# Later norm products, squares and weight sums at the start of the MLP's up projection; first down weights in another buffer and the last convolution behind them

## The chip, the cores and the metric

The kernel runs on one core of a Trainium2 chip. The metric is the device time of one execution in microseconds (us). TensorE is called PE here, its weight loads PEld, VectorE DVE, ScalarE ACT, GpSimd POOL; SP is the queue that issues nearly all DMAs. All engines run side by side, each through its own instructions in a fixed order, and wait for each other by semaphores.

## The reference, cut to what matters

One decoder layer runs on 1024 prompt tokens and 8 single new tokens, 1032 columns in all. Its first part (a norm, an input projection, two recurrent mixers, an output projection and the residual add, giving `x`) is touched only at its very end. Its second part is a gated MLP:

```
def rmsnorm(x, w):
    y = x * rsqrt(mean(x * x, axis=-1) + EPS)
    return y * w

x = x + concat([o_a, y]) @ w['w_out']            # 2048 -> 1024
h = rmsnorm(x, w['norm2_w'])
gate, val = split(h @ w['w_up'], 2)              # 1024 -> 2 x 2816
gate, buf = causal_dwconv(gate, buf_f, w['ffn_conv_w'], w['ffn_conv_b'])   # width 3
x = x + (silu(gate) * val) @ w['w_down']         # 2816 -> 1024
```

All of it is float32.

## The kernel before

**Layout.** Channels lie on the 128 partitions and tokens on the free axis, so `x` is 8 tiles of 128 x 1032. The tokens are cut into two halves of 516 columns, each of two quarters of 258 (`QW`). A float32 product is made of three rounded ones (high x high, low x high, high x low), so every operand has to be split first: ACT rounds it into a high tile (`wh`, `uh`, `ah`) and DVE subtracts to get the low tile (`wl`, `ul`, `al`).

**End of the output projection.** `out_job` (L1197) adds four products to `x` for each pair of channel tiles `m`; in the last pass over the second half DVE writes the finished piece `y_` into a small tile (tag `us`, a pool of 10 buffers), and `final` (L1248) stores it, squares it on ACT and adds the square to `rst` (tile `n2r`) on POOL. `rst` holds the sum of squares of each token over the 8 channel tiles.

**Norm.** `set_norm(i, c)` (L1307) sums `rst` over the partitions for one quarter by a PE product with ones (tile `n2ms`), and turns it into the reciprocal root with one ACT and three DVE instructions (L736 to L739). For the second half the scale is not put on the operands: it is multiplied onto the up projection's results (`p4` on DVE, `p3` on POOL).

**Up projection.** It runs in 22 steps `j` (`FT`), one for each 128 gate and 128 value channels. Each step uses a Strassen-like scheme of 7 products (`p1` to `p7`) for each token half, 12 matmuls to a product. The operands of a half, sums and differences of `x` quarters, are made once by `set_of(i)` (L1320): `comb` adds, `put` rounds and subtracts (L1349, L1350). The weights of a step are loaded by `up_load` (L1403), which also makes four sums of them (L1419, tile `wt`; POOL from step 1 on), and are split by `up_split` (L1428). `Up.p1` to `Up.p7` take the results out of PSUM; `p4` of a half may have to wait there for `p7`. `up_close` (L1513) then runs the convolution of width 3 (`conv_tail`, one ACT and two DVE instructions of 1048 columns, L354 and L356), the SiLU on ACT, and the product with `val`, and stores the step's result to DRAM (`act_d`).

**Order.** PE's instructions stand in the order in which the program issues them. All others are put into their queue by a list scheduler that works from the emission order, so a change in the emission moves rows on several engines. `tick()` is called after each matmul; `after(n, work)` emits `work` n matmuls later; `spread` emits the pieces of a generator at intervals of n matmuls. Step 0 (`ups(0, ...)`) runs all 7 products of the first half and then all 7 of the second, in the order `FIRST` = p1, p2, p4, p6, p5, p7, p3; the second half's operands are still being made while it runs. Later steps alternate the halves in the order p1, p6, p5, p7, p2, p4, p3.

**PSUM.** Products p1, p7, p3 (tiles `ua`) use 3 banks; p2, p4, p6, p5 (tiles `ub`) and one of the norm products use 4 others. A product waits until the bank it is given has been emptied.

**Down projection.** `act_load` (L1558) brings a stored result back (SP) and splits it. For each group of `RND` = 4 of the 22 channel tiles and each pair of output tiles, `wload` (L187) loads 512 KB of `w_down` into `ws`, rounds to `wh` (L199) and subtracts to `wl` (L201); then 8 products of 12 matmuls each (tile `dn`) follow, each added to its `x` tile by DVE (L1601). The tags `wh` and `wl` exist with two buffers each in two pools, `tmp` and `wpool`: in a step `up_split` uses `tmp` for its first two pairs of weights and `wpool` for its last two, and `wload` uses `wpool`.

## Time and profile before

| what | value |
|---|---|
| runs | 1733.5, 1734.27 (median), 1738.18 us |
| profiled execution, its own time | 1734.45 us |
| its span (first to last instruction) | 1732.7 us |
| mean granted PE clock | 0.994 |
| output projection ends, up step 0 begins | 999.4 us |
| up step 1 begins | about 1029.7 us |
| down projection begins | 1454.9 us |

The span is cut into 40 equal slices below; a digit is the busy share in tenths, PEclk the clock that was granted to PE in tenths.

```profile
## 2 busy tenths in 40 slices
PE   7999999999999999999999989999999998999997
...
DVE  6667756565575555466655877666766677444445
ACT  7567686345364444446334554334333334111114
POOL 2102132120121112011232367666666662000002
```

The slice is 43.3 us long, so the digits 8 on PE stand at 996 to 1040 us (start of the up projection) and at 1429 to 1473 us (start of the down projection). DVE's largest digits stand in the first of these.

### The profile page before, as it was taken

To read this page: it belongs to the slowest core of one execution; us is meant where nothing else is said; L and a number is where in the kernel's file an instruction comes from. 1 tells how busy PE (TensorE), PEld (TensorE's weight loads), DVE (VectorE), ACT (ScalarE), POOL (GpSimd) and SP (SyncE) were. 2 spreads that over 40 slices of the span, in tenths; PEclk is the share of its full clock that TensorE was granted. 3 is DMA by queue.
4 is the path that set the end of the run, shared out by engine and by line. 5 is a ranking of instruction groups with operands and counts; after the bars stand their busy time and mean duration, and the time that the engine had idled before them with its cause. 6 is when DMAs were issued, how large, how long until landed. Compare 5 with 4: busy or idle time off the path is not lost. (4 is left out here: it accounts for less than half of the span.)

```text
span 1732.7 us, 38321 instructions
## 1 busy us (share of the span) xinstructions
PE 1698.1 (98%) x16056; PEld 1654.6 (95%) x16056; DVE 1084.4 (63%) x1968; ACT 777.6 (45%) x1432; POOL 489.8 (28%) x503
## 2 busy tenths in 40 slices
PE   7999999999999999999999989999999998999997
PEld 7899998999999999999999989999999998999997
DVE  6667756565575555466655877666766677444445
ACT  7567686345364444446334554334333334111114
POOL 2102132120121112011232367666666662000002
PEclk9999999999999999999999999999999999999999
DMA  5354334643434334426358612222222227322212
GB/s 169 66 129 112 105 92 141 174 132 99 130 89 136 114 93 129 122 90 198 113 154 273 210 57 87 74 75 74 86 82 91 74 74 273 102 68 94 81 61 99
DMA packets 251000, 200.22 MB, mean 116 GB/s; under 512 B 48029, under 2 KB 222613, under 8 KB 250810
## 3 DMA queue, kind: packets, MB, share of 16 engines
q1 hardware_dynamic: 250538, 197.67, 37.5%
q8 instruction: 126, 2.06, 0.5%
q14 instruction: 48, 0.39, 0.1%
q0 software_dynamic: 288, 0.10, 0.0%
HBM read 155.16 MB, written 46.95 MB: 117 GB/s over the span
## 5 line engine op out<-in xcount | busy, mean ns | idle before, releaser
L93 PE MATMUL mm<-hl,wh 128*128 128x344 f32 x1248 | 405.1, 325 | 0.3 <-issue 0.3
L93 PE MATMUL mm<-hh,wh 128*128 128x344 f32 x1248 | 404.9, 325 | 0.0
L93 PE MATMUL mm<-hh,wl 128*128 128x344 f32 x1248 | 401.9, 322 | 0.0
L93 PEld LDWEIGHTS mm<-hl,wh 128*128 128x128 f32 x1248 | 235.4, 189 | 4.7 <-issue 4.2
L93 PEld LDWEIGHTS mm<-hh,wh 128*128 128x128 f32 x1248 | 235.5, 189 | 3.1 <-issue 2.5
L93 PEld LDWEIGHTS mm<-hh,wl 128*128 128x128 f32 x1248 | 235.6, 189 | 1.8 <-issue 1.7
L199 ACT CAST wh<-ws 128x1024 fp32r<-128x1024 f32 x96 | 100.6, 1048 | 247.7 <-PE dn L93 138.0
L93 PE MATMUL ub<-uh,wh 128*128 128x258 f32 x704 | 200.7, 285 | 1.5 <-DVE nt L737 0.8
L93 PE MATMUL ub<-ul,wh 128*128 128x258 f32 x704 | 199.7, 284 | 0.0
L93 PE MATMUL ub<-uh,wl 128*128 128x258 f32 x704 | 199.3, 283 | 0.0
L93 PE MATMUL dn<-ah,wl 128*128 128x256 f32 (+1 forms) x640 | 181.2, 283 | 5.8 <-DVE wl L201 5.8
L93 PE MATMUL dn<-ah,wh 128*128 128x256 f32 (+1 forms) x640 | 181.6, 284 | 0.0
L93 PE MATMUL dn<-al,wh 128*128 128x256 f32 (+1 forms) x640 | 180.7, 282 | 0.0
L201 DVE TENSOR_TENSOR wl<-ws,wh 128x1024 fp32r<-128x1024 f32 x88 | 115.4, 1312 | 95.1 <-ACT wh L199 94.5
L93 PE MATMUL ua<-uh,wh 128*128 128x258 f32 x528 | 150.0, 284 | 1.3 <-DVE val L1501 1.3
L93 PE MATMUL ua<-ul,wh 128*128 128x258 f32 x528 | 149.1, 282 | 0.6 <-DVE ul L1350 0.6
L93 PE MATMUL ua<-uh,wl 128*128 128x258 f32 x528 | 149.3, 283 | 0.0
L93 PE MATMUL mm<-mh,wh 128*128 128x258 f32 x512 | 145.6, 284 | 0.1
L93 PE MATMUL mm<-ml,wh 128*128 128x258 f32 x512 | 145.1, 283 | 0.0
L93 PE MATMUL mm<-mh,wl 128*128 128x258 f32 x512 | 144.7, 283 | 0.0
L1439 DVE TENSOR_TENSOR wl<-wt,wh 128x512 fp32r<-128x512 f32 x88 | 89.4, 1036 | 77.0 <-ACT wh L1438 77.0
L1601 DVE TENSOR_TENSOR x<-x,dn 128x256 f32<-128x256 f32 (+1 forms) x160 | 67.1, 421 | 110.0 <-PE dn L93 110.0
(368 smaller groups left out, 4029.9 us busy)
## 6 DMA issues: line engine op xcount, KB each, us to landing
ws<-in_w_in_dram SPq DMA_DIRECT2D x52, 512.0 KB
ws<-in_w_up_dram SPq DMA_DIRECT2D x44, 512.0 KB
ws<-in_w_out_dram SPq DMA_DIRECT2D x24, 512.0 KB
act_d<-val SPq DMA_DIRECT2D x22, 516.0 KB
al<-act_d SPq DMA_DIRECT2D x22, 516.0 KB
ws<-in_w_down_dram SPq DMA_DIRECT2D x22, 512.0 KB
ml<-mix_d SPq DMA_DIRECT2D x48, 172.0 KB
csb<-cs_d SPq DMA_DIRECT2D x32, 256.0 KB
```

Of the source, the lines that this page charges most:

```text
L93: PE.matmul(out, lhsT, rhs, start=start, stop=stop)
L199: A.copy(wh[:, :n], ws[:, :n])
L201: V.tensor_tensor(wl[:, :n], ws[:, :n], wh[:, :n].bitcast(F32), op=ALU.subtract)
L1439: V.tensor_tensor(lo[:, cs], sums[name], hi[:, cs].bitcast(F32), op=ALU.subtract)
L1601: V.tensor_tensor(xT[m + i][:, cs], xT[m + i][:, cs], ps, op=ALU.add)
```

## The change

It has seven parts.

1. `final` gets `held`: for the second half and the channel tiles m = 5, 6, 7 the piece is not squared at once but put on the list `unsquared`. `squares()`, new, squares each in place on ACT and adds it to `rst` on POOL; it is emitted piece by piece, from 50 matmuls into step 0 on, every 8. These six pieces so need no tile of their own for the square.
2. `set_norm` of the second half is emitted 150 instead of 93 matmuls into step 0.
3. In the second `set_of`, the subtraction for `p5` goes from POOL to DVE and stands behind the POOL additions for `p3`.
4. `up_load` no longer makes the weight sums; `up_sums`, new, does. For step 1 it is called after product 8 instead of 5 (counted from 0); the other steps are as before.
5. Step 21's `up_close` is put off: `closing` holds it until the first `wload` of the down projection has been emitted.
6. The first `wload` of the down projection takes `wh` and `wl` from `tmp` instead of `wpool` (`beside`).
7. The loads of the second group's activations (`nxt`) are emitted behind that too.

```diff
-    def wload(src, kt, m=P, kept=None, hold=None):
+    def wload(src, kt, m=P, kept=None, hold=None, beside=None):
...
-        wh = wpool.tile([P, KT * P], F32R, tag="wh", bufs=2, name=nm("wh"))
+        wh = (beside or wpool).tile([P, KT * P], F32R, tag="wh", bufs=2, name=nm("wh"))
...
-        pool, tag, b = (tmp, "wk", 1) if again and nkept[0] % 3 == 1 else (wpool, "wl", 2)
+        pool, tag, b = (tmp, "wk", 1) if again and nkept[0] % 3 == 1 else (beside or wpool, "wl", 2)
...
-                            final(m + i, y_, ts_)
+                            final(m + i, y_, ts_, hf and m + i > 4)
...
-    def final(m, x_, ts_):
+    def final(m, x_, ts_, held=False):
...
+        elif held:
+            unsquared.append((x_, ts_))
...
+    unsquared = []
+
+    def squares():
+        for x_, ts_ in unsquared:
+            A.activation(x_, x_, AF.Square)
+            G.tensor_tensor(rst[:, ts_], rst[:, ts_], x_, op=ALU.add)
+            yield
...
             up_load(0)
+            up_sums(0)
...
-            yield from put("p5", [s_[0]], "hT", G)
             yield from comb(s_, G, two(s_[1]), a2, ALU.add)
+            yield from put("p5", [s_[0]], "hT")
             yield from put("p3", [s_[2]], "big")
...
-        (g1, g2), (v1, v2) = ((t[:, :512], t[:, 512:]) for t in ws)
+        wparts[j] = ws
+
+    def up_sums(j):
+
+        (g1, g2), (v1, v2) = ((t[:, :512], t[:, 512:]) for t in wparts[j])
         sums = {}
...
             if n == (2 if j else 5) and j + 1 < FT:
                 up_load(j + 1)
+            if n == (2 if j else 8) and j + 1 < FT:
+                up_sums(j + 1)
...
-        up_close(j, us_[0])
+        if j < FT - 1:
+            up_close(j, us_[0])
+        else:
+            closing.append(lambda: up_close(j, us_[0]))
+
+    closing = []
...
-        after(93, lambda: (set_norm(1, 0), set_norm(1, 1)))
+        after(50, lambda: spread(squares(), 8))
+        after(150, lambda: (set_norm(1, 0), set_norm(1, 1)))
...
-            nxt = [act_load(r0 + RND + k) for k in range(min(RND, FT - r0 - RND))]
+            if r0:
+                nxt = [act_load(r0 + RND + k) for k in range(min(RND, FT - r0 - RND))]
             for m in range(0, KT, 2):
-                wh, wl = wload(w_down[0, rows, m * P:(m + 2) * P], nk, 2 * P)
+                wh, wl = wload(w_down[0, rows, m * P:(m + 2) * P], nk, 2 * P, beside=None if r0 or m else tmp)
+                if closing:
+                    closing.pop()()
+                    nxt = [act_load(RND + k) for k in range(RND)]
```

**Where the instructions stand now: DVE at the start of the down projection.** First DVE's rows of before, from the last result of the gate branch in step 21 on. `al` and `ah` are activations of the down projection, `wl` its weights, `fcv` the convolution, `val` the value branch, `dn` the down products, `x` the sums that they are added to.

```order
L1496 TENSOR_TENSOR fext_17766<-fext_17766,n2r_795 128x8
L1155 TENSOR_TENSOR al_18012<-al_18012,ah_18011 128x1032
L1501 TENSOR_TENSOR val_17767<-us_17817,ua_17959 128x258
L356 SCALAR_TENSOR_TENSOR fcv_17988<-fext_17766,vcol,fcv_17988 128x1048
L1501 TENSOR_TENSOR val_17767<-us_17832,ua_17973 128x258
...
L1155 TENSOR_TENSOR al_18017<-al_18017,ah_18016 128x1032
L201 TENSOR_TENSOR wl_18038<-ws_18036,wh_18037 128x1024
L1520 TENSOR_TENSOR val_17767<-val_17767,fext_17766 128x1032
L201 TENSOR_TENSOR wl_18160<-ws_18158,wh_18159 128x1024
L1155 TENSOR_TENSOR al_18022<-al_18022,ah_18021 128x1032
L1601 TENSOR_TENSOR x_2295_18042<-x_2295_18042,dn_18044 128x256
```

The same stretch of DVE in the changed kernel:

```order
L1511 TENSOR_TENSOR fext_17760<-fext_17760,n2r_795 128x8
L1155 TENSOR_TENSOR al_17998<-al_17998,ah_17997 128x1032
L1516 TENSOR_TENSOR val_17761<-us_17811,ua_17953 128x258
L356 SCALAR_TENSOR_TENSOR fcv_18008<-fext_17760,vcol,fcv_18008 128x1048
L1516 TENSOR_TENSOR val_17761<-us_17826,ua_17967 128x258
...
L1155 TENSOR_TENSOR al_18017<-al_18017,ah_18016 128x1032
L1628 TENSOR_TENSOR x_2289_18036<-x_2289_18036,dn_18038 128x256
L1535 TENSOR_TENSOR val_17761<-val_17761,fext_17760 128x1032
L1628 TENSOR_TENSOR x_2289_18036<-x_2289_18036,dn_18052 128x256
L1628 TENSOR_TENSOR x_2289_18036<-x_2289_18036,dn_18066 128x256
...
L201 TENSOR_TENSOR wl_18154<-ws_18152,wh_18153 128x1024
```

The row left out behind the second `val` is the second instruction of the convolution, which reads like the first. The first down weights (`wl_18038` before) are gone from here; where they stand now shows the next piece, DVE's rows while step 21 is at its products p6 and p7:

```order
L1155 TENSOR_TENSOR al_17983<-al_17983,ah_17982 128x1032
L1480 TENSOR_TENSOR us_17826<-us_17792,ub_17813 128x258
L201 TENSOR_TENSOR wl_18004<-ws_18002,wh_18003 128x1024
L1155 TENSOR_TENSOR al_17988<-al_17988,ah_17987 128x1032
L1488 TENSOR_TENSOR us_17871<-us_17811,ua_17858 128x258
L1488 TENSOR_TENSOR us_17888<-us_17826,ua_17875 128x258
L1155 TENSOR_TENSOR al_17993<-al_17993,ah_17992 128x1032
```

So `wl_18004` has moved from behind both convolution rows and the fifth `al` row to a place behind the first `al` row; four `al` rows, the two convolution rows and the eleven rows of step 21's last results that stood ahead of it now stand behind it. The weights of the second pair of output tiles (`wl_18154`) have moved the other way, from ahead of the first eviction of a `dn` product to behind the fourth.

**DVE in step 0, where the second half's operands are made.** Before, from the weights of p3 on (`ul` is the low part of an operand, `sm` a sum for one, `us`, `fext` and `val` are evictions of products, `nt` belongs to the norm):

```order
L1439 TENSOR_TENSOR wl_12247<-ws_11945,wh_12246 128x512
L1357 TENSOR_TENSOR sm_12311<-x_1088_9765,x_1170_10507 128x516
L1350 TENSOR_TENSOR ul_12282<-x_1088_9765,uh_12281 128x516
L1357 TENSOR_TENSOR sm_12323<-sm_12311,x_1088_9765 128x516
L1350 TENSOR_TENSOR ul_12296<-x_1153_10370,uh_12295 128x516
L1481 TENSOR_TENSOR fext_12250<-us_12274,ub_12276 128x258
...
L1465 TENSOR_TENSOR us_12338<-us_12274,ub_12318 128x258
...
L1350 TENSOR_TENSOR ul_12382<-sm_12370,uh_12381 128x1032
L1473 TENSOR_TENSOR us_12385<-us_12338,ua_12365 128x258
L1489 TENSOR_TENSOR fext_12250<-us_12385,ub_12300 128x258
L1501 TENSOR_TENSOR val_12251<-us_12338,ua_12402 128x258
L737 SCALAR_TENSOR_TENSOR nt_12428<-n2ms_12426,n2r_795 128x258
```

In the changed kernel, the same stretch:

```order
L1360 TENSOR_TENSOR ul_12264<-x_1088_9765,uh_12263 128x516
L1454 TENSOR_TENSOR wl_12229<-ws_11945,wh_12228 128x512
L1367 TENSOR_TENSOR sm_12293<-x_1088_9765,x_1170_10507 128x516
...
L1496 TENSOR_TENSOR fext_12232<-us_12256,ub_12258 128x258
...
L1367 TENSOR_TENSOR sm_12305<-sm_12293,x_1088_9765 128x516
...
L1480 TENSOR_TENSOR us_12320<-us_12256,ub_12300 128x258
...
L1360 TENSOR_TENSOR ul_12370<-sm_12345,uh_12369 128x1032
L1360 TENSOR_TENSOR ul_12362<-sm_12293,uh_12361 128x1032
L1488 TENSOR_TENSOR us_12373<-us_12320,ua_12349 128x258
L1504 TENSOR_TENSOR fext_12232<-us_12373,ub_12282 128x258
L1516 TENSOR_TENSOR val_12233<-us_12320,ua_12382 128x258
L1496 TENSOR_TENSOR fext_12232<-us_12415,ub_12417 128x258
```

The second piece of p1's operand (`ul_12282`, now `ul_12264`) stands ahead of the weights and of a sum instead of behind them; `ul_12362`, the operand of p5 that POOL made before, stands behind the operand of p3; and the norm's `nt` row, which followed `val` directly, stands six rows below the last one shown, behind the first four weight splits of step 1.

**PE in step 0, the norm products of the second half.** Before, between the ninth and the tenth matmul of the second half's p1 (`ua_12416`):

```order
L93 MATMUL ua_12416<-ul_12282,wh_12022 128x258
L93 MATMUL ua_12416<-uh_12281,wl_12023 128x258
L93 MATMUL n2ms_12426<-n2r_795,ones 128x258
L93 MATMUL n2ms_12433<-n2r_795,ones 128x258
L93 MATMUL ua_12416<-uh_12281,wh_12022 128x258
```

In the changed kernel, in the middle of the second half's p7 (`ua_12494`):

```order
L93 MATMUL ua_12494<-ul_12253,wh_12222 128x258
L93 MATMUL ua_12494<-uh_12252,wl_12223 128x258
L93 MATMUL n2ms_12501<-n2r_795,ones 128x258
L93 MATMUL n2ms_12508<-n2r_795,ones 128x258
L93 MATMUL ua_12494<-uh_12252,wh_12222 128x258
```

The two products have moved past the rest of p1 and the whole of p2, p4, p6 and p5. What they read (`n2r`) is finished on POOL by six additions, which before alternated with the operand sums and the weight sums of step 1, and do so now in another order, with the weight sums one addition earlier and nothing of p5 behind them.

## The prediction

> **What bounds the kernel now.** I read the page's busy shares first, then PE's waits over the up and down projections, then the timelines around the longest waits.
>
> ```profile
> PE 1698.1 (98%) x16056; PEld 1654.6 (95%) x16056; DVE 1084.4 (63%) x1968; ACT 777.6 (45%) x1432; POOL 489.8 (28%) x503
> ...
> PE dn L93 <- DVE wl L201: 5.8, 1, 5.8
> PE n2ms L93 <- POOL n2r L1254: 3.1, 2, 2.7
> PE ua L93 <- DVE val L1501: 1.3, 1, 1.3
> PE ub L93 <- DVE nt L737: 0.8, 1, 0.8
> PE ub L93 <- DVE us L1465: 0.7, 1, 0.7
> PE ua L93 <- DVE ul L1350: 0.6, 1, 0.6
> ```
>
> PE is the bound, busy for 98% of the span, and the change takes no matmul away. So it can only win what PE waits for, and what follows from a wait. The six rows (total, times, longest) are all that PE waits for between 940 and 1480 us: 12.3 us. Five of them lie in the up projection's first 55 us, one at the start of the down projection.
>
> **The start of the down projection (parts 5 to 7).** PE's timeline, then DVE's and ACT's:
>
> ```profile
> 1454.85 0.28 PE L93 MATMUL dn<-ah,wh 128*128 128x256 f32 x1
> 1454.97 0.28 PE L93 MATMUL dn<-al,wh 128*128 128x256 f32 x1
> 1461.08 0.58 PE L93 MATMUL dn<-ah,wl 128*128 128x256 f32 x1 [5.83 <-DVE wl L201]
> ...
> 1465.72 0.29 PE L93 MATMUL dn<-ah,wl 128*128 128x256 f32 x1
> ...
> 1453.30 1.23 DVE L1155 TENSOR_TENSOR al<-al,ah 128x1032 fp32r<-128x1032 f32 x1
> ...
> 1456.36 1.30 DVE L356 SCALAR_TENSOR_TENSOR fcv<-fext,vcol,fcv 128x1048 f32<-128x1048 f32 x1
> 1457.59 2.30 DVE L1155 TENSOR_TENSOR al<-al,ah 128x1032 fp32r<-128x1032 f32 x1
> 1459.81 1.21 DVE L201 TENSOR_TENSOR wl<-ws,wh 128x1024 fp32r<-128x1024 f32 x1
> ...
> 1441.16 1.06 ACT L1154 CAST ah<-al 128x1032 fp32r<-128x1032 f32 x1 [2.12 <-DMA al<-act_d]
> ...
> 1451.21 1.05 ACT L1154 CAST ah<-al 128x1032 fp32r<-128x1032 f32 x1 [3.72 <-DMA al<-act_d]
> 1452.17 1.05 ACT L199 CAST wh<-ws 128x1024 fp32r<-128x1024 f32 x1
> ```
>
> The pitch of matmuls is 0.12 us (1454.85 to 1454.97). The third matmul needs `wl`. ACT had rounded the weights at 1453.2, but on DVE two convolution rows and an `al` of the next group stood ahead. The stall costs 1461.08 - 1454.97 - 0.12 = 5.99 us. Behind it matmuls run slowly:
>
> ```profile
> 1014.60:1022.10 7.50, 6.45 (x25) 5.56 (x26) 6.55 (x8) 4.39 (x8) 5.38 (x3) 0.54 0.01 2
> 1461.10:1465.90 4.80, 4.80 (x23) 4.80 (x24) 3.67 (x4) 0.04 (x1) 0.00 (x0) 0.52 0.78 240
> ```
>
> These rows of stages end with the granted clock, DMA share and GB/s: the clock is about half after both long waits. From 1461.08 to 1465.72 PE makes 21 steps in 4.64 us, where 21 x 0.12 = 2.52 would do: 2.12 us lost. Together 8.1 us.
>
> In the changed order the first `wl` stands behind the first `al` of step 21's third product. Its `wh` buffer (in `tmp`) was read last by p6, ten products of 12 x 0.12 = 1.44 us ahead of 1454.85, so it is free at 1440.4. The weights were asked for ahead of that first activation (which ACT had at 1441.16), so ACT rounds them at about 1442.2 to 1443.2, and DVE, which had 1.17 us of idle time before its second `al`, subtracts by 1445.0. The next thing PE needs is the fourth activation: its `al` ended at 1454.5 (1453.30 + 1.23). The third weights' load is now asked for at about 1445, ahead of that activation's load, and 512 KB at the 421 GB/s of this stage take 1.25 us:
>
> ```profile
> 1450.00:1454.00 4.00, 4.00 (x35) 4.00 (x34) 2.26 (x6) 2.51 (x3) 1.16 (x2) 1.00 1.03 421
> ```
>
> So ACT has it at 1452.5 instead of 1451.21, `al` is ready by about 1454.8, and PE wants it at 1454.85 + 10 x 0.12 = 1456.05: no wait. Behind it DVE has the two convolution rows, the fifth `al`, then the first eviction (about 1460). The eighth down product reuses the second's bank: PE gets there at 1454.85 + 7 x 1.42 = 1464.8, DVE has evicted it by about 1461.8. The second weights, now behind four evictions, are split by about 1463.8 and wanted at 1466.2. All three hold with 1.2 to 3 us to spare, so I take the whole 8.1 us; its ends are 8.1 and, with a fresh wait of 3 us plus half clock (2.1), 3.0.
>
> **Step 0 (parts 1 to 4).** PE and DVE:
>
> ```profile
> 1011.38 0.39 PE L93 MATMUL ua<-ul,wh 128*128 128x258 f32 x1 [0.59 <-DVE ul L1350]
> 1014.62 0.72 PE L93 MATMUL n2ms<-n2r,ones 128*128 128x258 f32 x2 [2.73 <-POOL n2r L1254]
> 1015.67 1.23 PE L93 MATMUL n2ms<-n2r,ones 128*128 128x258 f32 x2 [0.33 <-POOL n2r L1254]
> 1016.34 0.78 PE L93 MATMUL ua<-uh,wh 128*128 128x258 f32 x1
> ...
> 1018.25 0.55 PE L93 MATMUL ub<-uh,wh 128*128 128x258 f32 x1 [0.70 <-DVE us L1465]
> ...
> 1025.26 0.39 PE L93 MATMUL ub<-uh,wh 128*128 128x258 f32 x1 [0.79 <-DVE nt L737]
> ...
> 1006.24 1.16 DVE L1350 TENSOR_TENSOR ul<-x,uh 128x516 fp32r<-128x516 f32 x1 [1.13 <-ACT uh L1349]
> ...
> 1017.70 0.41 DVE L1465 TENSOR_TENSOR us<-us,ub 128x258 f32<-128x258 f32 x1
> 1018.03 2.37 DVE L1350 TENSOR_TENSOR ul<-sm,uh 128x1032 fp32r<-128x1032 f32 x2
> 1020.32 0.41 DVE L1473 TENSOR_TENSOR us<-us,ua 128x258 f32<-128x258 f32 x1
> 1020.76 0.42 DVE L1489 TENSOR_TENSOR fext<-us,ub 128x258 f32<-128x258 f32 x1
> ...
> 1019.34 3.34 POOL L1350 TENSOR_TENSOR ul<-sm,uh 128x1032 fp32r<-128x1032 f32 x1 [2.12 <-ACT uh L1349]
> ```
>
> PE waits for the norm sums at 1011.7, for banks at 1018.25, and p5 of the second half starts at 1025.26, because its bank was the norm product's, emptied by `nt`. But DVE works from 1006.24 to 1021.18 with 0.2 us of pauses: it makes the operands and empties the banks. Taking the norm product away leaves PE waiting for DVE. In the new order p4 of the second half needs the bank of the first half's p6 (`us`, ended 1018.1) and p5 that of the first half's p4 (`fext`, ended 1021.18). DVE gets one more `ul` of 1032 columns (2.37 / 2 = 1.2 us, in place of POOL's 3.34). Against that, ACT has fewer squares ahead of its roundings: 0.3 us ahead of p5's weights, and most of the 1.13 us pause at 1006.24 (an eviction, a square and a rounding on ACT, one square less, and one rounding ahead of the next `x`). I put the end of `fext` at 1021.2, as before; its ends are 1020.0 and 1022.4. So p5 starts at 1021.2 instead of 1025.26: 4.1 us won. The norm products, which PE had paid by then, follow: 1016.34 - 1014.62 less the wait of 0.33 = 1.4 us at half clock, 0.7 at full. PE also meets one long wait on the way. Step 0 begins at 999.44, so the second half's p1 begins 84 x 0.12 us later, at 1009.5; its low operand now stands earlier on DVE and is there. p2 waits until about 1012 for DVE to empty a bank and is over at 1013.6; p4's bank is free at about 1016.9: 3.3 us. If the clock halves there, as it did after 2.73 us at 1014.62, p4 and p6 take 2 x 2.6 instead of 2 x 1.44 us and p5 begins at 1022.1: 0.9 us less. So 4.1 - 0.7 - 0.9 = 2.5 us; ends 0 (DVE late by 1.2, clock still slow in p7 and p3) and 4.
>
> [...]
>
> The 1.3 us for `val` stands at 1052.79, in step 2:
>
> ```profile
> 1052.79 0.39 PE L93 MATMUL ua<-uh,wh 128*128 128x258 f32 x1 [1.27 <-DVE val L1501]
> ...
> 1035.91 0.68 DVE L1439 TENSOR_TENSOR wl<-ws,wh 128x512 fp32r<-128x512 f32 x1
> ...
> 1040.96 1.85 POOL L1419 TENSOR_TENSOR wt<-ws 128x512 f32<-128x512 f32 x1 [6.75 <-DMA ws<-in_w_up_dram]
> ```
>
> DVE is late there because step 2's weights were: their buffer came free with the `wl` at 1035.91, the load landed at 1040.96, POOL's sums and DVE's splits followed. In the new order that `wl` stands ahead of the convolution, at about 1033, 3 us or more earlier, while PE is 2.5 us earlier. So the wait shrinks by about 1.0 us; ends 0 and 1.4. The squares and the later weight sums I cost at nothing: POOL finishes `n2r` at about 1018, and PE reads it at 1023.5. An in-place square also waits for the store of its piece:
>
> ```profile
> 1007.76 0.32 SPq L1248 DMA_DIRECT2D x_d<-x  x1
> ```
>
> This is the last store's issue. ACT comes to its square at about 1010.7 and has nothing else to do before DVE's sum at 1014.3; a store that landed later than that would delay p6's operand one for one.
>
> **Sum.** 8.1 + 2.5 + 1.0 = 11.6 us. The profiled execution took 1734.45 us (its span 1732.7), so 1722.9; it stands 0.2 above the median of 1734.27. I say **1723.0**.
>
> **The rivals.**
> - *Only the down projection wins.* DVE, not the norm, bounds step 0; with its extra `ul` at the late end and half clock until step 1, the 2.5 and the 1.0 are gone. For it speaks DVE's unbroken row of work, against it the pause at 1006 and the bank that p5 no longer waits for. 1734.45 - 8.1 = 1726.3. Chance 0.18.
> - *The wait at the down projection comes back on the fourth activation,* whose load is now behind 512 KB more. If it lands 5.6 us later than before instead of 1.25, `al` is ready at 1451.21 + 5.6 + 1.05 + 1.23 = 1459.1 and PE stalls 3 us, with the slow clock behind it: 8.1 falls to 3.0, giving 1728. [...] Chance 0.09, a third of it within 0.3% of before.
> - *Slower: the third weights block ACT.* Their rounding now stands on ACT ahead of the fifth activation's and of the last SiLU, and DVE has `al` and `val` ahead of its evictions. Each us by which that load lands after about 1459 delays the second weights past 1466.2 and PE with them. It must land after 1459 + 11.6 = 1470.6, 25 us after it is asked for, to cost more than all is worth; at 1480 it would be 1744. Against it stands how fast a load of this size landed there:
>
> ```profile
> 1446.65 0.43 SPq L1561 DMA_DIRECT2D al<-act_d  x1
> ```
>
>   That is the fourth activation's; ACT had it 4.6 us later, at 1451.21, with other loads in flight. Chance 0.03.
> - *Nothing moves.* The waits named are not the ones that bind, and another engine's stand right behind both: 1733. Against it: DVE's `wl` starts the moment the `al` ahead of it ends. Chance 0.04.
>
> **How the numbers follow.** The forecast, with 1721 to 1725, has 0.66. Measurements of this kernel can tell about 0.3% (5.2 us) from no change. Faster by more: 0.66 + 0.18 + 0.06 = 0.90; within: 0.03 + 0.04 = 0.07; slower 0.03. The range for 8 in 10 goes from 1720.5 (8.1 + 4 + 1.4 us won, rounded down) to 1728, where the returned wait ends.
>
> **What would show it.** Right: no wait of `dn` for `wl` over 0.5 us, and a granted clock near 1.0 after the start of the down projection; `wl` L201 on DVE before its second down `al`; up step 1 beginning 2 to 3 us earlier; a wait of about 3 us in step 0, now for `us`, and p5 waiting for `fext` instead of `nt`; under 0.6 us left in step 2. Wrong: a new `dn` wait for `al`, `ah` or `x`, or a step 1 that begins when it did.

## The result, and the profile after

| | before | changed |
|---|---|---|
| runs | 1734.69 us median (1733.5 to 1738.18, 6 runs) | 1724.72 us median (1721.74 to 1725.88, 6 runs) |
| ratio | | 0.9936, 95% interval 0.9923 to 0.9949 |
| profiled execution, its own time | 1734.45 | 1724.76 |
| its span | 1732.7 | 1723.1 |
| up projection's first matmul | 999.44 | 998.94 |
| from there to the first down matmul ("up") | 455.41 | 454.39 |
| from the first down matmul to the end ("down") | 277.85 | 269.77 |

The changed kernel is faster by 0.5 to 0.8%, inside the forecast's range and 1.7 us above its point. By the three last rows, 8.08 us came from the down projection, 1.02 from the up projection and 0.50 from what lies ahead of it, 9.6 us of the span in all. Where the up projection begins is scatter: over the profiles of this study it begins anywhere from 997.9 to 1001.1 us, with the same work ahead of it but for the squares that part 1 moves. The span is given to 0.1 us, so "down" is good to 0.05 us.

The page's busy shares and slices after:

```profile
PE 1692.9 (98%) x16056; PEld 1650.3 (96%) x16056; DVE 1087.7 (63%) x1969; ACT 777.3 (45%) x1432; POOL 485.8 (28%) x502
...
PE   7999999999999999999999989999999999999997
```

Of the two slices in which PE had an 8, the one at the start of the down projection is a 9 now; the one at the start of the up projection is still an 8. PE's waits between 940 and 1480 us (total, times, longest) say why:

```profile
PE ub L93 <- DVE us L1480: 3.5, 1, 3.5
PE ua L93 <- DVE val L1516: 1.7, 1, 1.7
PE ua L93 <- DVE wl L1454: 1.1, 1, 1.1
PE ub L93 <- DVE x L1235: 0.5, 1, 0.5
PE ub L93 <- DVE fext L1496: 0.2, 1, 0.2
```

The 5.8 for `wl` L201 is gone and nothing of the down projection has taken its place. In the up projection 6.5 us of waits in five rows have become 7.0 in five others. At the down projection PE's, DVE's and ACT's timelines, and a row of PE's first 12 us with the granted clock (third number from the end):

```profile
1453.33 0.28 PE L93 MATMUL dn<-ah,wh 128*128 128x256 f32 x1
1453.45 0.28 PE L93 MATMUL dn<-al,wh 128*128 128x256 f32 x1
1453.56 0.28 PE L93 MATMUL dn<-ah,wl 128*128 128x256 f32 x1
...
1442.14 1.22 DVE L201 TENSOR_TENSOR wl<-ws,wh 128x1024 fp32r<-128x1024 f32 x1
1443.34 1.23 DVE L1155 TENSOR_TENSOR al<-al,ah 128x1032 fp32r<-128x1032 f32 x1
...
1452.23 1.23 DVE L1155 TENSOR_TENSOR al<-al,ah 128x1032 fp32r<-128x1032 f32 x1 [0.37 <-ACT ah L1154]
...
1459.40 0.41 DVE L1628 TENSOR_TENSOR x<-x,dn 128x256 f32<-128x256 f32 x1
...
1451.15 1.05 ACT L1154 CAST ah<-al 128x1032 fp32r<-128x1032 f32 x1 [5.31 <-DMA al<-act_d]
...
1453.33:1465.33 12.00, 12.00 (x104) 12.00 (x103) 11.45 (x16) 5.11 (x6) 2.31 (x1) 1.00 0.75 280
```

The third matmul follows the second by one pitch, PE makes 104 matmuls in 12 us at full clock (35 before, below), and the first `wl` stands ahead of DVE's second `al`, done 10 us before it is wanted. The fourth activation is the rival that came nearest: ACT has it 2.2 us ahead of the first down matmul instead of 3.6, and its `al` is over at 1453.46, 1.1 us before PE wants it (1453.33 + 10 x 0.12). The forecast had left it 1.2 us.

### The profile page after: what moved, and what is told of

It reads as the page before. It is cut to its first block, busy times and chain, and to the rows that moved or that the text cites. A ratio compares the mean times of both kernels' runs of the same rounds, so it can differ in the third digit from the quotient of the medians.

```text
span 1723.1 us, 38317 instructions
## 1 busy us (share of the span) xinstructions
PE 1692.9 (98%) x16056; PEld 1650.3 (96%) x16056; DVE 1087.7 (63%) x1969; ACT 777.3 (45%) x1432; POOL 485.8 (28%) x502
## 5 line engine op out<-in xcount | busy, mean ns | idle before, releaser
L201 DVE TENSOR_TENSOR wl<-ws,wh 128x1024 fp32r<-128x1024 f32 x88 | 115.5, 1313 | 94.4 <-ACT wh L199 94.3
L93 PEld LDWEIGHTS ub<-uh,wh 128*128 128x128 f32 x704 | 133.7, 190 | 4.7 <-ACT uh L1359 3.6
L1454 DVE TENSOR_TENSOR wl<-wt,wh 128x512 fp32r<-128x512 f32 x88 | 88.0, 1019 | 73.2 <-ACT wh L1453 72.9
```

What stands on the lines that cost most here:

```text
L93: PE.matmul(out, lhsT, rhs, start=start, stop=stop)
L201: V.tensor_tensor(wl[:, :n], ws[:, :n], wh[:, :n].bitcast(F32), op=ALU.subtract)
L1454: V.tensor_tensor(lo[:, cs], sums[name], hi[:, cs].bitcast(F32), op=ALU.subtract)
```

## The experiments

All of them are variants of the two kernels. "Half clock" in the table is how long PE was granted half of its clock in the 18 us from 11 us after the up projection's first matmul: 2 x (1 - clock) x 18, by a row of 18 us as shown further down; the rows give the clock to 0.01, so it is good to 0.2 us. Times with + are counted from that matmul, and p7 and p6 are the starts of those products.

| kernel | p7 of second half | step 1's first p6 | half clock | step 2's weight sums begin | wait for `val` in step 2 | up | down |
|---|---|---|---|---|---|---|---|
| before | +27.4 | +33.1 | 6.8 | +41.5 | 1.3 | 455.41 | 277.85 |
| buffer_only | +27.3 | +33.1 | 10.1 | +41.2 | 1.3 | 455.41 | 269.66 |
| close_only | +27.4 | +33.1 | 10.1 | +41.5 | 1.3 | 455.34 | 270.70 |
| changed | +25.0 | +31.8 | 3.2 | +40.6 | 1.7 | 454.39 | 269.77 |
| sums_early | +25.9 | +32.5 | 6.8 | +39.3 | none | 453.30 | 270.24 |
| up_only | +25.8 | +32.4 | 6.8 | +39.4 | none | 453.45 | 278.22 |
| norm_93 | +27.0 | +32.7 | 3.2 | +41.5 | 1.3 | 455.01 | 270.04 |
| p5_on_pool | +26.0 | +32.8 | 6.8 | +41.5 | 1.6 | 455.32 | 269.73 |
| no_held | +25.8 | +32.4 | 10.1 | +39.2 | none | 453.17 | 269.76 |
| busy_up | +24.8 | +31.8 | 0 | +39.2 | 0.5 | 453.16 | 269.83 |
| busy_no_held | +24.6 | +31.6 | 0 | +39.1 | 0.6 | 453.13 | 270.61 |

Single profiles scatter. "Up" differs by 1.1 us between the changed kernel and sums_early, which have one and the same order, and "down" goes from 269.66 to 270.61 over eight kernels whose instructions stand in the same order there; in these eight the 97th down matmul begins 11.39 us after the first, so that scatter arises later.

### Which part pays at the down projection: buffer_only, close_only, up_only

buffer_only is before with part 6 alone; the call is shown, the three lines inside `wload` are those of the change:

```diff
-                wh, wl = wload(w_down[0, rows, m * P:(m + 2) * P], nk, 2 * P)
+                wh, wl = wload(w_down[0, rows, m * P:(m + 2) * P], nk, 2 * P, beside=None if r0 or m else tmp)
```

> Only part 6 (first down weights in the other buffer) is put into the kernel before; the convolution stays ahead in the emission. The list scheduler then puts every row where it stands with parts 5 to 7. Stages: up = first matmul of up step 0 to first down matmul (before 455.4 us, changed 454.4), down = from there to the end of the span (before 277.9, changed 269.8). Theory A, the buffer alone moves the weights' split ahead of the convolution and the two other parts do nothing: up 455.4, down 269.8, no wait of dn, clock 1.0 behind the start, about 8.1 us faster than before (ratio 0.9953). Rival B, the gain needs step 0's changes too (another arrival time of the loads): down 272 or more, or a new wait of dn.

Measured: 1726.69 us median, ratio 0.9948 (0.9934 to 0.9962). PE waits for nothing at the start of the down projection, and "down" is 269.66 us, 8.19 less than before: all of the gain there. From the last steps of the up projection on, every engine's instructions stand in the same order as in the changed kernel, which has parts 5 and 7 as well, so beside part 6 these two do nothing.

close_only is before with parts 5 and 7 and without part 6:

```diff
-        up_close(j, us_[0])
+        if j < FT - 1:
+            up_close(j, us_[0])
+        else:
+            closing.append(lambda: up_close(j, us_[0]))
...
+                if closing:
+                    closing.pop()()
+                    nxt = [act_load(RND + k) for k in range(RND)]
```

> Parts 5 and 7 without part 6: the last convolution and the next group's activations are emitted behind the first down weights, which stay in the old buffer, free only when p4's product ends, 2.9 us before the down projection. The weights' split now stands behind the fourth activation's on DVE, ahead of the convolution. Theory A, it is the place on DVE that counts: wl ready at about the first down matmul + 1.0 us (before: + 6.1), so a wait of about 0.9 us, too short to lower the clock: down 277.9 - 5.2 - 2.1 = 270.6, up 455.4, ratio 0.996. Rival B, the buffer counts by its own: DVE or ACT is late with the weights all the same, wait 3 us or more and the clock at half behind it, down 275 or more.

Measured: 1727.46 us, ratio 0.9948 (0.9935 to 0.996). One wait is left:

```profile
PE dn L93 <- DVE wl L201: 0.8, 1, 0.8
```

The split now stands ahead of the convolution but behind the fourth `al`. The granted clock is 1.00 in every row of 1 us from 1440 to 1480 us, so behind this wait it did not fall. "Down" is 270.70, 7.15 less than before. The convolution on DVE was what the weights stood behind. Either edit takes them past it, and part 6 also takes away the wait of 0.8 us that is left here.

up_only is the changed kernel without parts 5 to 7 (the diff is that of parts 1 to 4, as shown in the section on the change).

> Parts 1 to 4 alone. Theory A, both ends of the change add up: up 454.4 (1.0 us won), down 277.9 with the old wait of 5.8 us for wl: about 1.0 us faster, ratio 0.9994, the interval holds 1. Rival B, the larger difference of the medians (11 us against 9.6 us in the profiles) is step 0's, and the profile shows too little of it: ratio 0.998 or less. Rival C, as predicted, 3.5 us.

Measured: 1733.44 us, ratio 0.9991 (0.9982 to 1.0), so 1.6 us by the ratio, with no change at the edge of the interval. The wait for `wl` is back (6.1 us), "down" is 278.22. "Up" is 453.45: this order of the up projection was worth 1.96 us in this profile and 1.02 in the changed kernel's.

### The price of the slow clock at the down projection: busy_down

Before, with 45 matmuls that nobody reads ahead of the first down product, in the time in which PE waited:

```diff
+                    if not (r0 or m or i):
+                        idle = bank("idle", "nx")[:, :QW]
+                        for _ in range(45):
+                            mm(idle, acts[0][0][:, :P], acts[0][0][:, :QW])
```

> The kernel before with 45 matmuls whose result nobody reads ahead of the first down matmul, 5.4 us at 0.12 us each, where PE waits. Theory A, the slow matmuls behind the wait are the price of the idle time: with PE kept busy the pitch of the down matmuls stays 0.12 us and the clock 1.0; from the last up matmul to the end of the span 275 instead of 277.9 us (2.1 us for the clock, and up to 0.6 where the split is ready before the 45 are through). Rival B, they are slow because of the loads and splits that run beside them (DMA share 0.78): the pitch is 0.21 for some 4 us all the same and at most 0.6 us is won.

Measured: 1732.35 us in one run, beside 1735.53 for before. PE's timeline of busy_down, and a row of the first 12 us:

```profile
1454.88 5.60 PE L93 MATMUL idle<-ah 128*128 128x258 f32 x45
1460.32 0.28 PE L93 MATMUL dn<-ah,wh 128*128 128x256 f32 x1
...
1454.88:1466.88 12.00, 11.43 (x95) 11.22 (x94) 10.76 (x12) 4.29 (x6) 2.29 (x1) 1.00 0.77 280
```

The same row of before:

```profile
1454.85:1466.85 12.00, 6.17 (x35) 5.96 (x34) 10.35 (x11) 4.21 (x5) 2.27 (x1) 0.72 0.78 283
```

PE still starts on the weights at 1461.29 (1461.08 before), but the clock is 1.00 instead of 0.72. From the first matmul behind the up projection to the end it takes 1730.6 - 1454.88 = 275.72 instead of 277.85: 2.13 us won without shortening the wait for data. Of these, 1.85 are there by the 97th down matmul (17.72 us after 1454.88, where before has 19.57 after 1454.85); the other 0.28 come in the last 14 us, where profiles scatter. As the weights also came 0.18 later, the slow clock cost about 2.0 us, close to the forecast's 2.12. The slow matmuls behind the stall are a price of PE's idleness, not of the loads and splits beside them, which ran here as well (DMA share 0.77, before 0.78).

### The same program again: sums_early

The changed kernel without part 4. Its instructions stand in the same order as the changed kernel's on every engine, so part 4 by itself moves nothing, and this run is a second sample:

```diff
-            if n == (2 if j else 8) and j + 1 < FT:
+            if n == (2 if j else 5) and j + 1 < FT:
                 up_sums(j + 1)
```

> The changed kernel without part 4 (step 1's weight sums emitted after product 5 again). Every engine's instructions stand in the same order as in the changed kernel, so this is a second sample of the same program. Theory (what scatters between profiles is the phase of half-clock stretches and the moment at which step 2's weights land, not the order): the wait for `us` ahead of the second half's p4 is 3.5 us again, PE runs at half clock for a whole multiple of 3.4 us (one such in the changed kernel, two where only the up projection's parts were made), p7 of the second half begins at +25.0 with one and about +25.8 with two; step 2's weights land between 39.2 and 40.6 us after the first matmul, and its wait for `val` is between 0 and 1.7 us; the up projection takes 453.2 to 454.4 us. Rival (part 4 did something): the wait for `us` or for the p3 weights is another, or the up projection takes over 455 us.

Measured: 1726.32 us in one run, "up" 453.30. The waits are the same to 0.1 us as in the changed kernel (3.5 for `us`, 1.1 for the weights), but for step 2's, which is gone. Two things scatter. First the clock; the row of 18 us of the changed kernel:

```profile
1009.94:1027.94 18.00, 14.35 (x101) 13.84 (x102) 16.70 (x24) 9.80 (x19) 7.87 (x8) 0.91 0.00 1
```

of sums_early:

```profile
1012.06:1030.06 18.00, 14.34 (x93) 13.84 (x94) 16.71 (x24) 9.25 (x18) 7.85 (x8) 0.81 0.00 1
```

and of no_held (below):

```profile
1009.97:1027.97 18.00, 14.34 (x81) 13.58 (x80) 16.77 (x24) 9.01 (x17) 8.21 (x8) 0.72 0.00 1
```

2 x 0.09 x 18 = 3.2, 2 x 0.19 x 18 = 6.8, 2 x 0.28 x 18 = 10.1 us at half clock. By rows of 1 us it is 3.42, 6.84 and 10.24, the second twice and the third three times the first to 0.02, so I count them as one, two and three stretches of 3.42. Behind the same wait of 3.46 us PE got one such stretch in the changed kernel's profile and two in sums_early, p7 began 0.9 us later and step 1's p6 0.7 us later. Second, step 2's weights; POOL's first sum of them in the changed kernel, and PE's wait at the end of the chain:

```profile
1039.49 1.29 POOL L1434 TENSOR_TENSOR wt<-ws 128x512 f32<-128x512 f32 x1 [5.80 <-DMA ws<-in_w_up_dram]
...
1051.29 0.39 PE L93 MATMUL ua<-uh,wh 128*128 128x258 f32 x1 [1.69 <-DVE val L1516]
```

and in sums_early:

```profile
1040.40 1.29 POOL L1434 TENSOR_TENSOR wt<-ws 128x512 f32<-128x512 f32 x1 [4.51 <-DMA ws<-in_w_up_dram]
```

That is +40.6 and +39.3 us. The second of the two loads had been issued at +35.7 and +35.8; it landed 1.2 us later in the one than in the other. PE was 0.7 us later in sums_early as well, and the wait vanished. So the slow clock and the late load do not add up: the later PE is in step 0, the less it waits in step 2.

### The parts at the up projection: norm_93, p5_on_pool, no_held

norm_93 is the changed kernel without part 2:

```diff
-        after(150, lambda: (set_norm(1, 0), set_norm(1, 1)))
+        after(93, lambda: (set_norm(1, 0), set_norm(1, 1)))
```

> The changed kernel without part 2: the second half's norm products are emitted after 93 matmuls again, the squares stay late. In the changed kernel the second half's p7 begins 25.0 us after the up projection's first matmul, up step 1's first p6 31.8 us after it, and the up projection takes 454.4 us. Theory (the norm products were a wait of their own, and part 2 is what took it away): POOL finishes the sum of squares 18.1 us after the first matmul in the changed kernel, so PE waits for it from about 12.6 to 18.1; then come the norm products and the rest of p1 and all of p2 at a slow clock, and p7 begins at about +27.4, step 1's p6 at about +33.4, the up projection takes about 456 us. Rival (DVE's row of operands and evictions bounds the whole of step 0, the norm products only filled a wait that is there anyway): p7 begins at +25.0 to +25.7 and the up projection takes 454.4 us or less.

Measured: 1724.75 us in one run. PE's waits by its timeline:

```profile
1013.06 0.70 PE L93 MATMUL n2ms<-n2r,ones 128*128 128x258 f32 x2 [1.86 <-POOL n2r L1263]
1015.93 1.23 PE L93 MATMUL n2ms<-n2r,ones 128*128 128x258 f32 x2 [2.17 <-POOL n2r L1263]
...
1023.30 0.39 PE L93 MATMUL ub<-uh,wh 128*128 128x258 f32 x1 [0.56 <-DVE nt L737]
```

The wait for the norm sums is back, 4.0 us, and ends at +18.1 as expected; p5 waits for `nt` again. p7 begins at +27.0, near the +27.4 of the theory, and "up" is 455.01 (456 expected), within 0.4 us of before. So without part 2 little of the gain is left in this profile. But the 4.0 us that it takes away bring only 2.0 at p7 and, with the norm products themselves behind that, 0.9 at step 1.

p5_on_pool is the changed kernel without part 3:

```diff
+            yield from put("p5", [s_[0]], "hT", G)
             yield from comb(s_, G, two(s_[1]), a2, ALU.add)
-            yield from put("p5", [s_[0]], "hT")
             yield from put("p3", [s_[2]], "big")
```

> The changed kernel without part 3: POOL makes the low operand of the second half's p5 again (3.3 us there), DVE has 1.2 us less ahead of the eviction `fext` that frees p5's bank. Theory (behind the wait for `us` PE's slow clock bounds, not DVE): p7 still begins at +25.0 (within 0.3), the up projection takes 454.4 us within 0.6. Rival (DVE bounds there): p7 at about +24.0, the up projection 453.4 us. Second rival (POOL is late with p5's operand or with the two additions that free the bank for p3): a wait of PE for `ul` or `val` ahead of p5 or p7, p7 at +26 or later.

Measured: 1727.25 us in one run, "up" 455.32. The theory had p7 at +25.0; it came at +26.0, with two slow stretches (+25.8 and +25.9 in the two samples with as many). But the operand itself shows something else. DVE and POOL in p5_on_pool:

```profile
1018.81 4.57 DVE L1360 TENSOR_TENSOR ul<-sm,uh 128x1032 fp32r<-128x1032 f32 x2
...
1025.33 0.42 DVE L1516 TENSOR_TENSOR val<-us,ua 128x258 f32<-128x258 f32 x1 [1.16 <-POOL us L1490]
...
1019.67 2.61 POOL L1360 TENSOR_TENSOR ul<-sm,uh 128x1032 fp32r<-128x1032 f32 x1 [1.67 <-ACT uh L1359]
```

DVE in the changed kernel:

```profile
1017.81 3.51 DVE L1360 TENSOR_TENSOR ul<-sm,uh 128x1032 fp32r<-128x1032 f32 x3
```

Two subtractions beside POOL's take 4.57 us, three without it 3.51. The second of the two starts at 1019.95, while POOL's runs, and lasts 3.43 us. So beside the other edits the move to DVE shortens DVE's row by 1.1 us, where I had charged it 1.2. Without part 3 what follows is 1.0 us later: `val` at +25.4 (1025.33) instead of +24.3, behind it step 2's load (its second half is issued at +36.8 instead of +35.7), and "up" is within 0.1 us of before. The load itself took as long as in the changed kernel's profile (4.7 and 4.8 us from there to POOL's first sum), so the 0.93 us between the two are not its scatter. By these single profiles parts 2 and 3 are both needed.

no_held is the changed kernel without part 1:

```diff
-                            final(m + i, y_, ts_, hf and m + i > 4)
+                            final(m + i, y_, ts_)
```

> The changed kernel without part 1: the last squares are made at once, in tiles of their own. DVE then has the split of the first half's p3 weights back ahead of the second operand of p1 and the sum, as before. Theory (part 1 only shuffles DVE's row, whose length sets when the second half's p4 gets its bank): the wait of 1.1 us for the p3 weights is gone, the wait for `us` ahead of the second half's p4 is longer by as much, 4.5 us; p7 begins at +25.0 (within 0.4), the up projection takes 454.4 us (within 0.6). Rival (the slipped p3 weights cost 1.1 us): p7 at +23.9, up projection 453.3 us. Second rival (the squares on ACT delay the roundings, so part 1 is what shortened DVE's row): p7 at +26, up projection 455.4 us.

Measured: 1723.59 us in one run, "up" 453.17. The wait for the p3 weights is gone, as expected, and PE waits for an operand (0.57 us) and at the next two banks instead, where 4.5 us for `us` alone were expected. PE in no_held:

```profile
1013.99 0.55 PE L93 MATMUL ub<-uh,wh 128*128 128x258 f32 x1 [2.21 <-DVE fext L1496]
1017.79 0.55 PE L93 MATMUL ub<-uh,wh 128*128 128x258 f32 x1 [0.88 <-DVE us L1480]
```

DVE is through with the eviction that frees p5's bank at +23.0 (+23.2 in the changed kernel), so its row is as long, and the second half's p4 begins at +18.8 (+19.1). But p7 begins at +25.8, outside the +25.0 expected, behind three slow stretches; and "up" is 1.2 us less than expected, as step 2 has no wait. By this run part 1 wins nothing.

### What bounds step 0 now: busy_up, busy_no_held

busy_up is the changed kernel with 26 unread matmuls in PE's wait for `us`:

```diff
+            if not j and i and name == "p4":
+                idle = bank("idle", "nx")[:, :QW]
+                u = usets[1]["p1"][0]
+                for _ in range(26):
+                    mm(idle, u.rearrange("p k t -> p (k t)")[:, :P], u[:, 0, :])
```

> The changed kernel with 26 more matmuls, whose results nobody reads, ahead of the second half's p4, where PE waits 3.5 us for `us` and then runs at a granted clock of 0.72 for 4 us. They take about 3 us of that wait. Theory (the slow clock behind the wait costs step 0 its 1.5 us: 35 steps from 1018.03 to 1023.95 took 5.9 us, where 36 x 0.12 = 4.3 would do): p4, p6 and p5 run at full clock until p5 needs the bank that `fext` frees at about +23.2; p7 begins at about +24.6 instead of +25.0, since DVE is next, and the norm products behind it take 0.7 us less at full clock; up step 1's p6 at +31.0 instead of +31.8. Rival (only the wait counts, the clock behind it costs nothing): all as in the changed kernel, +25.0 and +31.8. Second rival (the clock alone bounds): p7 at +23.5, p6 at +29.6.

Measured: 1723.49 us in one run, "up" 453.16. PE in busy_up:

```profile
1014.28 3.29 PE L93 MATMUL idle<-uh 128*128 128x258 f32 x26
...
1017.92 0.36 PE L93 MATMUL ub<-uh,wh 128*128 128x258 f32 x1 [0.35 <-DVE us L1480]
...
1022.05 0.39 PE L93 MATMUL ub<-uh,wh 128*128 128x258 f32 x1 [1.01 <-DVE fext L1504]
```

The clock stays at 1.00 in every row of 1 us of step 0 (in the changed kernel the row from 1018.03 to 1024.03 has the 0.72 of the expectation, 6 us and not 4; its first 4 us have 0.64), and p5 now waits 1.01 us for `fext`: DVE is next, at once. p7 begins at +24.8 instead of +25.0, close to the +24.6 of the theory; step 1's p6 has not moved (+31.8), against the theory's +31.0. What holds it is DVE again. DVE and PE in busy_up, then DVE and PE in the changed kernel:

```profile
1028.58 0.42 DVE L1488 TENSOR_TENSOR us<-us,ua 128x258 f32<-128x258 f32 x1
1029.05 0.39 PE L93 MATMUL ua<-uh,wh 128*128 128x258 f32 x1
...
1028.70 0.42 DVE L1488 TENSOR_TENSOR us<-us,ua 128x258 f32<-128x258 f32 x1
...
1029.18 0.39 PE L93 MATMUL ua<-uh,wh 128*128 128x258 f32 x1
```

This `us` empties the bank of the second half's p7, which step 1's second product needs. It stands behind the norm's six DVE rows, which part 2 has moved there, and it is over at +30.2 in both kernels; PE goes on within 0.1 us of it. No run moves it, so what it costs is not measured. The slow clock costs step 0 only 0.2 us in the changed kernel's profile; where there are two stretches it costs more (p7 at +25.9 in sums_early, which has the same order).

busy_no_held joins no_held to 20 unread matmuls ahead of the second half's p2:

```diff
-                            final(m + i, y_, ts_, hf and m + i > 4)
+                            final(m + i, y_, ts_)
...
+            if not j and i and name == "p2":
+                idle = bank("idle", "nx")[:, :QW]
+                u = usets[1]["p1"][0]
+                for _ in range(20):
+                    mm(idle, u.rearrange("p k t -> p (k t)")[:, :P], u[:, 0, :])
```

> The changed kernel without part 1, and with 20 unread matmuls ahead of the second half's p2, where PE waits 2.2 us for `fext` and where the half-clock stretch of 10.2 us began in the run without part 1. Theory (behind the slow clock DVE's row is the next bound, and behind that step 2's weights): no granted clock below 1 in step 0; p7 of the second half begins at about +23.8 instead of +25.8, when DVE has emptied p5's bank (+23.0 without part 1, as there); but step 2's `val` is ready at +51.1 at the earliest, as its weights land no sooner, so PE waits there and the up projection still takes 453.2 to 454.4 us: 1723.5 to 1724.7 us in all. Rival (the clock bounded all of it): the up projection takes 451.5 us, 1722 us in all.

Measured: 1724.94 us median of 5, ratio 0.9936 (0.9923 to 0.995): the changed kernel's, to the fourth digit. The clock is 1.00 throughout, p7 comes at +24.6 (+23.8 expected: p5 begins at +23.1, as DVE allows, but takes its own 1.44 us before p7), and "up" is 453.13, within 0.1 us of the 453.2 to 454.4 of the theory, far from the 451.5 of the rival. Five variants end at 453.1 to 453.5, whatever their clock did. In the two of them with the clock held up, PE waits 0.5 and 0.6 us in step 2, for the weights that landed at +39.2 and +39.1; the other three come late enough not to wait. No version tried here beats the changed kernel measurably.

## Why the prediction was right, and where it was not

**The down projection: 8.1 forecast, 8.08 measured.** Both halves hold. The stall went with the place of `wl` on DVE (5.99), and busy_down shows that the slow matmuls (2.12 forecast, about 2.0 measured) were a price of the idle time. What I credited to three parts is one part's: part 6 alone gives 8.19, parts 5 and 7 alone 7.15. The cover that I named (activation, banks, second weights) held; the tightest had 1.1 us to spare.

**Step 0: 2.5 forecast, 1.3 measured at step 1's p6 in the changed kernel's profile, 0.6 and 0.7 in the two others of the same order.** The sign named for it, step 1 beginning 2 to 3 us earlier, did not come. The kind was right: the norm wait went, a wait for `us` came in its place (3.3 forecast, 3.46 measured), the clock fell behind it, and with the clock held up p5 waits for `fext`, not `nt` (busy_up). The step that failed is DVE's row: `us`, "free at about 1016.9", and `fext`, "at 1021.2, as before". I charged the extra `ul` (1.2) and set against it most of the pause of 1.13 us ahead of the second half's first `ul`. DVE in the changed kernel:

```profile
1004.43 0.75 DVE L1235 TENSOR_TENSOR x<-x,mm 128x258 f32<-128x258 f32 x2
1006.25 0.70 DVE L1360 TENSOR_TENSOR ul<-x,uh 128x516 fp32r<-128x516 f32 x1 [1.07 <-ACT uh L1359]
...
1008.59 1.12 DVE L1454 TENSOR_TENSOR wl<-ws,wh 128x512 fp32r<-128x512 f32 x1
...
1017.48 0.41 DVE L1480 TENSOR_TENSOR us<-us,ub 128x258 f32<-128x258 f32 x1
...
1021.69 0.42 DVE L1504 TENSOR_TENSOR fext<-us,ub 128x258 f32<-128x258 f32 x1
```

The pause is still there, 1.07 us. ACT's timeline shows what fills it:

```profile
1004.88 0.51 ACT L1239 ACTIVATE x<-x,vcol 128x258 f32<-128x258 f32 x1 [2.58 <-DVE x L1235]
1005.29 0.40 ACT L1262 ACTIVATE x<-x 128x258 f32<-128x258 f32 x1
1005.60 0.61 ACT L1359 CAST uh<-x 128x516 fp32r<-128x516 f32 x1
```

ACT had itself waited 2.58 us for DVE's `x`, so that fewer squares ahead of it on ACT brought nothing forward, and one held square stands right in the chain from `x` to `uh`.

`us` ends at +18.95 (before +18.67) and `fext` at +23.17 (before +21.74): 0.28 and the whole of the third `ul`, 1.14, later. That is 0.2 us past the late end that I had given `fext` (1022.4 - 999.44 = +22.96). From the up projection's first matmul the forecast had `us` at +17.5 and `fext` at +21.8, so they came 1.5 and 1.4 us later than that. PE made up part of it by luck: the one half-clock stretch began only 1.2 us into p4, so p4 and p6 took 4.38 us (+19.09 to +23.47) instead of the 5.2 charged, and p5 began 0.8 us later than forecast. In sums_early, with two stretches, p4 and p6 took 5.3. The other 0.4 lie behind p5: from there to step 1's p6 the changed kernel loses 1.05 us against before, where 0.7 was charged for the norm products. They took 0.87: around them PE makes two steps of p7 in 1.11 us (1024.54 to 1025.65) instead of 0.24.

The section on the profile before says that DVE's largest digits stand in the slice of step 0; its one 8 stands in the slice ahead of that (953 to 996 us), and step 0 has a 7. I also overlooked that the p3 weights, moved behind a `ul` on DVE as the order quoted ahead of the prediction shows, are wanted by PE in the first half; PE waits 1.10 us for them. That wait cost little by itself: without it (no_held) the second half's p4 begins 0.3 us earlier.

**Step 2: 1.0 won forecast; 0.4 lost in the changed kernel's profile, all of 1.3 won in the two other profiles of the same order.** The sign "under 0.6 us left" failed in the one and held in the two. The chain was right, the certainty was not. I read one landing time as given; the weights were asked for 1.9 us earlier and landed 1.0 to 2.2 us earlier. norm_93 and p5_on_pool, where they landed at +41.5 as before, have the wait.

**The sum.** The three profiles of the changed up order give 1.0, 2.0 and 2.1 us where 3.5 was forecast. With 1.0, 8.1 and the 0.5 of the earlier start the span fell by 9.6 us and the profiled execution's own time by 9.7 (1734.45 - 1724.76), against 11.6. The 0.5 were no part of the forecast, so that much of its nearness is luck. (Its working gives 1722.7 on the median, 0.3 below the 1723.0 that it says.) "Only the down projection wins" (1726.3) was the nearest rival: the measured median lies between it and the forecast, and the ratios of the changed kernel and of buffer_only overlap. So the times of the runs do not tell parts 1 to 4 from nothing; that they win 1 to 2 us is what three profiles show.

**The clock.** I took 0.9 us for a slow stretch behind the wait. The rows show half clock behind that wait in all three profiles of the order, for 3.2 us in the changed kernel's and 6.8 in the two others (each to 0.2). What decides between one stretch and two behind the same wait is not shown. In the changed kernel the clock fell when PE was at work again, at 1019.2; in sums_early it fell within the wait, at 1018.7, when PE's last matmul had begun only 2.3 us earlier (3.74 ahead of 1020.15, at 1016.41).

## What to carry to other kernels

A matmul that waits for a weight split is mended by where the split stands on its engine, and one more buffer can be what lets a list scheduler put it there; look for the one edit that moves the row before crediting the rest. Where an engine's row of work sets the end of a stage, removing another wait in it wins only up to that row: add up the row in the new order, and take off a pause only after seeing which engine waits for which in it. A gain that ends on a load's landing should carry a range from the start, since the same order gave 0 and 1.7 us of wait here.

## What the runs showed of the hardware that was not expected

- The granted clock was half for 3.2, 6.8 or 10.1 us by the rows of 18 us above, each to 0.2. By rows of 1 us it was 3.42 in the changed kernel (0.59, 0.50, 0.50 and 0.70 from 1019 to 1023), 6.84 in sums_early (0.85, six of 0.50 and 0.73 from 1018 to 1026) and 10.24 in no_held (0.66, nine of 0.50 and 0.72 from 1013 to 1024): one, two and three times the first, to 0.02. The length behind one and the same wait of 3.46 us differed between two profiles of one order. In rows of 1 us each the clock fell at 1019.2 in the changed kernel, 1.2 us behind the end of the wait, and in sums_early at 1018.7, 1.4 us ahead of its end (1020.15).
- Filling the wait with matmuls whose results nobody reads kept the clock at 1.00 behind it in all three kernels that did so (busy_down by its row of 12 us, busy_up and busy_no_held by rows of 18 us); without them these rows had 0.72 in before, 0.91 in the changed kernel and 0.72 in no_held.
- A DVE subtraction of 128 x 1032 beside a POOL subtraction of the same size took 3.43 us instead of 1.22, while POOL's took 2.61 (p5_on_pool). POOL's had begun first, at 1019.67, DVE's at 1019.95; DVE's ended at 1023.38, 1.10 us behind POOL's. Before, where DVE's began first (1019.17, POOL's 1019.34), it was POOL's that took 3.34, and DVE's took 1.22. Why the later one took so long in these two pairs is not shown.
